# Reordering block work, low halves and merges in projection B and the output projection, and giving modulation chunks their own buffer

## The chip, the cores and the metric

The kernel runs on one core of a Trainium2 chip. Its engines are TensorE (matmuls; PE in the profile, with PEld for weight loads), VectorE (DVE), ScalarE (ACT), GpSimd (POOL) and SyncE (SP), which issues most of the loads. The metric is the device time of one execution in microseconds. Lower is better.

## What is computed

One decoder block on a sequence of 512 rows with 1024 columns, in float32: a modulation vector, one wide input projection, two mixers (a gated MLP over chunks, and sparse attention), each with a projection, a merge, an output projection, and a SwiGLU FFN.

```python
mod = silu(c) @ w_ada + b_ada                 # shift1, scale1, gate1, shift2, scale2, gate2
h = rms_norm(x, norm1_g) * (1 + scale1) + shift1
a_u, a_v, q, k, v, qi, ki, wi, g_a, g_b = split(h @ w_in)
y_a = chunked_gmlp(gelu(a_u), gelu(a_v), ...)
y_b = dsa_attention(q, k, v, qi, ki, wi)      # top-k keys per query, softmax, values
merged = sigmoid(g_a) * (y_a @ w_proj_a) + sigmoid(g_b) * (y_b @ w_proj_b)
x = x + gate1 * (merged @ w_out)
h2 = rms_norm(x, norm2_g) * (1 + scale2) + shift2
f_g, f_u = split(h2 @ w_ffn_in)
x = x + gate2 * ((silu(f_g) * f_u) @ w_ffn_out)
return rms_norm(x, final_norm_g)
```

## The kernel before

**Split products.** Every float32 product is made of three matmuls on rounded parts: high x high, high x low, low x high (mm3, L51 to L55). So each weight block that arrives has its high half made by a ScalarE copy and its low half by a subtraction, mostly on VectorE. These two steps are the "prep" of a block (L95).

**The stream.** Weight blocks ("w") and modulation chunks ("m") stand in one hand-written list, `stream`. A chunk is 512 KB of w_ada, used by two VectorE products that add to an accumulator (mac, L171); four chunks make half a section, and 24 chunks (numbered 0 to 23 here) the three sections 2, 3 and 4. When a half is complete, sec_tasks (L364) makes its column sum: for sections 3 and 4 four transposes on TensorE, then a reduction and one or two tiny steps on VectorE (L383 to L393). ensure(upto) (L119) issues the loads of as many blocks ahead as room(i) allows, and preps up to the block named; get(i, ahead=2) preps two weight blocks beyond the one that is about to be used. Weight blocks land in a buffer with three slots (tag raw). Chunks land there too, except those marked mid, which have a buffer with one slot, the tile mraw with tag A2. Each engine takes its instructions in program order, and a tile that is to be written waits until the last reader of the tile that had the buffer before is done, even where that reader stands later in the program.

**The stages around the change**, in order of time: projection A (W_GA and W_PA: gate and projection groups 0 to 3 of mixer A, two blocks to a group), the attention loop with the gate groups W_GB in its gaps, projection B (W_PB, opt_b with pb_evac: groups PB0 to PB3 of two blocks each), the output projection, the second norm and the FFN.

**Output projection.** Its first half of the inner dimension is done as a seven-product scheme over blocks: the merged rows' blocks and their sums (A11, A12, A22, S1 to S4 in part[0], made by o_sum and split by o_m), and w_out's blocks and differences (B11, B12, B21, B22, T1 to T4, loaded by o_issue into oraw, made by o_sub and split by o_w). The list O_STEPS says which of these steps is done at each of the eight blocks of projection B; o_step runs one entry. The products (oprod, L1300) then run with bank copies between: seed copies an accumulator to a new bank, keep copies it to SBUF, add_kept adds it back. The second half of the inner dimension (W_O[0] to W_O[3], tile wx for the first two) follows as plain products, half of the rows after the other (L1335). W_O[0] and W_O[1] lie in the buffers of yb, the input of projection B.

**Second norm.** resid adds to the residual rows and squares them; row_rstd and norm2_x normalise two row blocks, one on VectorE and one on ScalarE (tile xn); norm2_T transposes them on TensorE (x2T), scales (h2f) and splits them (h, in HB). norm2_T(0) serves the first half of the rows, norm2_T(1) the second; the latter stands inside the first FFN group (tile pf), whose two weight columns are W_F[0] and W_F[1], four blocks together (WF0[0] to WF0[3]). s_issue(-2) and s_prep(-2) load and prepare the weights of the first of the later FFN groups; s_prep gives four pairs of a ScalarE step and VectorE steps (a0, d0 to a3, d3), named pre[0] to pre[3]. t_diff and t_split follow.

Of the kernel before, what the change touches and what calls it, by code (L numbers as in the profile page):

```python
# [9 lines left out]
F32 = mybir.dt.float32  # L10
# [6 lines left out]
S = 512  # L17
# [11 lines left out]
def block_kernel(ctx: ExitStack, tc: tile.TileContext, x, positions, w_ada, b_ada, w_in,  # L29
# [28 lines left out]
    stream, wseq, chunk = [], [], {}  # L58
# [7 lines left out]
        return len(stream) - 1  # L66

    def add_m(dma, fn, early=False, mid=True):
        stream.append(dict(kind="m", fn=fn, dma=dma, early=early, mid=mid and not early))
        return len(stream) - 1  # L70

    def issue(i):
        e = stream[i]
        if e["kind"] == "m" and e["early"]:
            k = mrot[0]
            mrot[0] += 1
            raw = s2pair(k % 8, F32).rearrange("p a n -> p (a n)")
        elif e["kind"] == "m" and e["mid"]:
            raw = mid.tile([128, 1024], F32, name="mraw", tag="A2", bufs=1)
        else:  # L80
            raw = base.tile([128, 1024], F32, name="raw", tag="raw", bufs=RAWB)
        e["raw"] = raw
        if e["kind"] == "m":
            e["dma"](raw)
            return
        k0, nk, n = e["kts"][0], len(e["kts"]), e["n"]
        src = e["src"][k0 * 128:(k0 + nk) * 128, :]
        e["view"] = lambda t: t[:, :nk * n].rearrange("p (j n) -> p j n", j=nk)
        v = e["view"](raw)
# [54 lines left out]
    def get(i, ahead=2):  # L144
        k = wseq.index(i)
        ensure(wseq[min(k + ahead, len(wseq) - 1)])
        return chunk[i]
# [75 lines left out]
                        sec_done.append((sec, half, tick[0] + 2, ah))  # L223
                yield dma, fn

    def group(src, c0, n=256, K=8, mods=None, pool=False, where=None, nm=1, mraw=True):
        ids = []
        for k0 in range(0, K, 4):
            ids.append(add_w(src, list(range(k0, min(K, k0 + 4))), c0, n,
                             P if pool == 2 or pool and k0 % 8 == 0 else V, where.pop(0) if where else None))  # L230
            for _ in range(nm):
                m = next(mods, None) if mods is not None else None
                if m is not None:
                    add_m(*m, mid=mods is mm_ and mraw)
        return ids
# [18 lines left out]
    W_GA, W_PA = [], []  # L254
    for g in range(4):
        W_GA.append(group(w_in, 4168 + 256 * g, mods=mm_, pool=2))
        W_PA.append(group(w_pa, 256 * g, mods=mm_ if g < 3 else None, pool=2))
    W_GB = [group(w_in, 5192 + 256 * g, pool=2 * (g == 1), mods=mm_ if g > 1 else None, mraw=False) for g in range(4)]
    stream[W_GB[1][0]]["lo"] = V
    W_PB = [group(w_pb, 256 * g, mods=mm_ if g < 3 else None, mraw=False) for g in range(4)]  # L260

    W_O = [add_w(w_o, [k0, k0 + 1], 512 * h, 512, V, where) for h, k0, where in
           ((0, 4, ("S2_2", "S2_3")), (0, 6, ("S2_6", "S2_7")), (1, 4, None), (1, 6, None))]
# [403 lines left out]

    qf = [base.tile([128, 2, S], F32, name=f"qf{g}", tag=f"X{g}", bufs=1) for g in range(4)]

    def opt_b(ids, K, rhs, banks, evac, per_chunk=None, post=None, midway=None):  # L670
        pb = [bank(b, "pb") for b in banks]
        for i in ids:
            if per_chunk:
                per_chunk()
            hi, lo = get(i)
            kts = stream[i]["kts"]
            for j, kt in enumerate(kts):
                for m in range(2):
                    cc = slice(m * 128, (m + 1) * 128)
                    mm3(pb[m], (hi[:, j, cc], lo[:, j, cc]), rhs[kt], kt == 0, kt == K - 1)  # L680
                if midway and j == 1:
                    midway()
            if i == W_PB[3][-1]:
                sec_tasks(True)
            if i == ids[-1]:
                evac(pb)
            if post:
                post()
            sec_tasks()
# [381 lines left out]

    mT, om, ow, oraw = {}, {}, {}, {}
    OM = {"A11": 0, "S1": 1, "S2": 2, "A12": 3, "S3": 0, "S4": 1, "A22": 2}
    OW = {"B11": ("k_hi", "k_lo"), "T1": ("v_hi", "v_lo"), "T2": ("G0", "G1"), "T4": ("k_hi", "k_lo")}

    def o_issue():
        for n, (name, kh, h) in enumerate((("B11", 0, 0), ("B12", 0, 1), ("B22", 1, 1), ("B21", 1, 0))):
            t = oraw[name] = mid.tile([128, 2, S], F32, name="oraw", tag=f"A{n}", bufs=1)
            SY.dma_start(t, w_o[kh * 256:kh * 256 + 256, h * 512:h * 512 + 512].rearrange("(j p) n -> p j n", p=128))

    def o_w(key, src):
        if key in OW:
            ow[key] = tuple(mid.tile([128, 2, S], F32R, name="ow", tag=t, bufs=1) for t in OW[key])
        else:
            ow[key] = tuple(base.tile([128, 2, S], F32R, name=t, tag=t, bufs=3) for t in ("hi", "lo"))
        split(*ow[key], oraw[src])

    def o_sub(o, a, b):
        V.tensor_sub(oraw[o], oraw[a], oraw[b])
# [6 lines left out]
    def o_m(key):  # L1096
        om[key] = tuple(base.tile([128, 2, 256], F32R, name="om", tag=f"S1_{OM[key] + 8 * e}", bufs=1) for e in range(2))
        split(*om[key], m_block(key))

    def o_sum(key):  # L1100
        if key == "S1":
            V.tensor_add(m_block("S1"), m_block("A21"), m_block("A22"))
        else:
            a, b = {"S2": ("S1", "A11"), "S4": ("A12", "S2"), "S3": ("A22", "S2")}[key]
            V.tensor_sub(m_block(key), m_block(a), m_block(b))

    def pb_evac(g):
        def ev(pb):
            for m in range(2):
                k = 2 * g + m  # L1110
                t, o = t512("mg"), part[k // 4][:, k % 4]
                V.tensor_mul(t, pb[m], gbt[g][:, m])
                V.tensor_add(o, o, t)
                if k >= 4:
                    mT[k] = tuple(base.tile([128, S], F32R, name="mt", tag=f"S1_{k + 8 * e}", bufs=1) for e in range(2))
                    A.activation(mT[k][0], o, AF.Copy)
            for k in range(2 * g, 2 * g + 2):
                if k >= 4:
                    V.tensor_sub(mT[k][1], part[1][:, k % 4], f(mT[k][0]))
        return ev  # L1120

    O_STEPS = [[lambda: o_w("B11", "B11")],
               [lambda: o_sub("B11", "B12", "B11"), lambda: o_w("T1", "B11")],
               [lambda: o_sub("B11", "B22", "B11"), lambda: o_sub("B12", "B22", "B12")],
               [lambda: o_sum("S1"), lambda: o_m("A11"), lambda: o_sum("S2"), lambda: o_m("S1"),
                lambda: o_w("T2", "B11")],
               [lambda: o_m("S2"), lambda: o_m("A12"), lambda: o_sum("S4")],
               [lambda: o_sum("S3")],
               [lambda: o_w("B21", "B21")], []]

    def o_step():
        for fn in O_STEPS.pop(0):
            fn()

    mbank[0] = 5
    o_issue()
    for g in range(4):
        opt_b(W_PB[g], 8, yb, ((2, 3), (0, 1), (6, 7), (0, 1))[g], pb_evac(g), None, o_step)
    sec_tasks(True)


# [167 lines left out]

    WF0 = W_F[0] + W_F[1]  # L1310
    oprod(0, "A11", "B11", True)
    o_w("T3", "B12")
    seed(O, OB, 1, 0)
    oprod(3, "S1", "T1", True)
    o_m("S3")
    keep(O, 3, None)
# [549 lines left out]
```

## Time and profile before

| | |
|---|---|
| three runs | 844.22, 846.72, 849.07 us; median 846.72 |
| profiled execution | 844.57 us; span from first to last instruction 842.8 us |
| busy in the span | PE 822.8, PEld 731.1, DVE 679.4, ACT 410.0, POOL 107.9 us |
| moved by DMA | 109.10 MB, mean 129 GB/s |
| projection B | TensorE from 396.1 to about 444 us of the span |
| output projection | to about 491 us |
| second norm and first FFN group | to about 518 us |

The profile is of one execution, and its times are microseconds from the span's start. In a row of a timeline stand start, duration, engine, line, operation, output and inputs with their shapes, the count, and in square brackets how long the engine had been idle and which engine's step ended that. In a row of the windows stand the stretch, its length, the busy time of each engine with its count of instructions, the granted TensorE clock and the share and rate of DMA. In a row of grouped lines the numbers behind the bar are the busy time in us, the mean duration in ns, and the idle time ahead of the group. In the list of waits they are the total in us, the number of waits and the longest. An engine that isn't the bottleneck may idle at no cost.

### The profile page before, as it was taken

The page shows a single profiled execution, that of the slowest core. Times are in us where ns is not written, and L with a number is a line of the kernel's source. Part 1 is how long each engine was busy: PE and PEld are TensorE (multiplying, and loading weights), DVE is VectorE, ACT ScalarE, POOL GpSimd, SP SyncE. Part 2 cuts the span into 40 slices and gives each one's busy share as a digit, 9 for nine tenths or more (in the row PEclk, how much of TensorE's full clock was granted, in tenths as well). Part 3 has the DMA queues.
Part 4 walks back from the last instruction along what each step waited for, and adds up shares of the span by engine and source line. Part 5 has one row for each costly group of instructions (what it writes and reads, how often), then busy time and mean ns, then how long its engine had stood idle before and what let it go on. Part 6 is the DMA issues. An engine that isn't in the chain of part 4 may idle for free.

```text
span 842.8 us, 12864 instructions
## 1 busy us (share of the span) xinstructions
PE 822.8 (98%) x4980; PEld 731.1 (87%) x4980; DVE 679.4 (81%) x1169; ACT 410.0 (49%) x714; POOL 107.9 (13%) x101
## 2 busy tenths in 40 slices
PE   7999999999999999999988999999999999999996
PEld 6888889988888888988866889999999999888885
DVE  7978799798899648886787779889998888985635
ACT  6664445322332236666335466555555555563322
POOL 2060022452353411000000000000000000000001
PEclk9999999999999999999999999999999999999998
DMA  9962262432345541056641402345543334142212
GB/s 300 310 186 79 87 200 77 126 100 83 120 141 186 196 150 51 26 190 196 209 131 51 150 26 76 102 153 165 168 160 104 101 100 149 52 145 98 83 50 100
DMA packets 95677, 109.10 MB, mean 129 GB/s; under 512 B 5616, under 2 KB 76272, under 8 KB 95616
## 3 DMA queue, kind: packets, MB, share of 16 engines
q1 hardware_dynamic: 92512, 101.37, 38.8%
q0 software_dynamic: 2384, 6.10, 2.0%
q8 instruction: 39, 0.64, 0.3%
q10 hardware_dynamic: 720, 0.82, 0.3%
q14 instruction: 22, 0.18, 0.1%
HBM read 105.90 MB, written 2.10 MB: 128 GB/s over the span
## 4 chain that ended last, share of the span: by engine, by line
PE 85%; DVE 8%; ACT 2%; DMA 2%; issue 1%; SPq 0%; POOL 0%; POOLq 0%; DVEq 0%; ACTq 0%
PE R L53 7%; PE pb L55 7%; PE R L54 7%; PE pb L53 7%; PE R L55 7%; PE pb L54 7%; PE pfo L55 4%; PE pfo L54 4%; PE pfo L53 4%; PE pav L54 2%; PE pav L53 2%; PE pav L55 2%; PE pgb L53 2%; PE pgb L54 2%; PE pgb L55 2%
## 5 line engine op out<-in xcount | busy, mean ns | idle before, releaser
L112 ACT ACTIVATE hi<-raw 128x1024 fp32r<-128x1024 f32 (+2 forms) x82 | 84.5, 1034 | 101.1 <-PE pfo L55 35.2
L116 DVE TENSOR_TENSOR lo<-raw,hi 128x1024 fp32r<-128x1024 f32 (+2 forms) x46 | 55.5, 1212 | 48.5 <-ACT hi L112 48.3
L116 POOL TENSOR_TENSOR lo<-raw,hi 128x1024 fp32r<-128x1024 f32 x29 | 72.9, 2517 | 127.6 <-ACT hi L112 122.0
L53 PE MATMUL pb<-h,hi 128*128 128x512 f32 x192 | 76.4, 398 | 0.0
L55 PE MATMUL pb<-h,lo 128*128 128x512 f32 x192 | 75.8, 395 | 0.0
L54 PE MATMUL pb<-hl,hi 128*128 128x512 f32 x192 | 75.8, 395 | 0.0
L55 PE MATMUL pfo<-hi,gs 128*128 128x512 f32 (+1 forms) x126 | 46.4, 369 | 0.0
L54 PE MATMUL pfo<-lo,gs 128*128 128x512 f32 (+1 forms) x126 | 46.4, 368 | 0.0
L53 PE MATMUL pfo<-hi,gs 128*128 128x512 f32 (+1 forms) x126 | 46.4, 368 | 0.0
L53 PE MATMUL R<-tb,sx 128*128 128x256 f32 x160 | 45.3, 283 | 0.5 <-ACT R L1618 0.5
L53 PE MATMUL R<-tb,hi 128*128 128x256 f32 x160 | 44.9, 281 | 0.2 <-ACT ps L1636 0.2
L54 PE MATMUL R<-tb,sx 128*128 128x256 f32 x160 | 45.1, 282 | 0.0
L55 PE MATMUL R<-tb,sx 128*128 128x256 f32 x160 | 45.0, 281 | 0.0
L55 PE MATMUL R<-tb,lo 128*128 128x256 f32 x160 | 44.8, 280 | 0.0
L54 PE MATMUL R<-tb,hi 128*128 128x256 f32 x160 | 44.6, 279 | 0.0
L55 PEld LDWEIGHTS pb<-h,lo 128*128 128x128 f32 x192 | 36.0, 188 | 8.8
L54 PEld LDWEIGHTS pb<-hl,hi 128*128 128x128 f32 x192 | 36.0, 188 | 8.3
L53 PEld LDWEIGHTS pb<-h,hi 128*128 128x128 f32 x192 | 36.0, 188 | 8.3
L177 DVE SCALAR_TENSOR_TENSOR acc<-mraw,cols,acc 128x512 f32<-128x512 f32 x38 | 32.6, 859 | 8.2 <-DMA mraw<-in_w_ada_dram 7.5
L54 PE MATMUL pav<-lo,h 128*128 128x256 f32 x128 | 35.8, 279 | 0.0
L53 PE MATMUL pav<-hi,h 128*128 128x256 f32 x128 | 35.7, 279 | 0.0
L55 PE MATMUL pav<-hi,hl 128*128 128x256 f32 x128 | 35.7, 279 | 0.0
(400 smaller groups left out, 2663.9 us busy)
## 6 DMA issues: line engine op xcount, KB each, us to landing
raw<-in_w_ffn_in_dram SPq DMA_DIRECT2D x44, 512.0 KB, 4.3
raw<-in_w_in_dram SPq DMA_DIRECT2D x40, 512.0 KB, 3.8
mraw<-in_w_ada_dram SPq DMA_DIRECT2D x22, 512.0 KB, 3.8
raw<-in_w_ffn_out_dram SPq DMA_DIRECT2D x17, 512.0 KB, 3.6
s<-in_w_ada_dram SPq DMA_DIRECT2D x30, 256.0 KB, 5.6
raw<-in_w_ada_dram SPq DMA_DIRECT2D x10, 512.0 KB, 4.5
raw<-in_w_proj_a_dram SPq DMA_DIRECT2D x8, 512.0 KB, 4.6
raw<-in_w_proj_b_dram SPq DMA_DIRECT2D x8, 512.0 KB, 3.9
```

Of the source, the lines that this page charges most:

```text
L53: T.matmul(o, wh, rh, start=start, stop=False, **kw)
L54: T.matmul(o, wh, rlo, start=False, stop=False, **kw)
L55: T.matmul(o, wlo, rh, start=False, stop=stop, **kw)
L112: A.activation(hi[:, :m], e["raw"][:, :m], AF.Copy)
L116: e["lo"].tensor_sub(lo[:, :m], e["raw"][:, :m], f(hi[:, :m]))
L177: V.scalar_tensor_tensor(o, w, cs[:, j:j + 1], o, op0=OP.mult, op1=OP.add)
```

## The change

- Chunks: projection A takes two more (16 instead of 14). The attention loop keeps four. Projection B has four instead of six, after PB0's second block, both blocks of PB1 and PB2's first; these four land in the buffer of k_hi (free after the last score product), no longer in the three raw slots.
- opt_b gets a step that runs between the matmuls of a block and the merge (before, o_step ran behind the merge), and an ahead for get: 2 for PB0 to PB2, 0 for PB3, so that no w_out block of the plain part is prepped in projection B.
- o_issue takes names: B11, B12 and B22 load at the same place as before into A1, A0 and A2; B21 loads into k_hi in the fifth entry of O_STEPS. B11's and T4's halves lie in k_lo and A3.
- O_STEPS is regrouped: T1 has an entry of its own, T2 and the sum S1 come first in the fifth, A11, S2 and S1 in the sixth, A12 and B21 in the last.
- Output projection: the seed of accumulator 1 stands ahead of o_w("T3"); W_O[0] and W_O[1] are prepped ahead of the product S3 x T3, W_O[2] ahead of A22 x T4.
- Second norm: WF0[2] is prepped inside norm2_T(0), its low half one step later, followed by s_issue(-2). WF0[3] is prepped behind norm2_x(1), and pre[0], pre[1] and pre[2] all follow it.

```diff
-        stream.append(dict(kind="m", fn=fn, dma=dma, early=early, mid=mid and not early))
+        stream.append(dict(kind="m", fn=fn, dma=dma, early=early, mid=not early and mid))
...
-            raw = mid.tile([128, 1024], F32, name="mraw", tag="A2", bufs=1)
+            raw = mid.tile([128, 1024], F32, name="mraw", tag=e["mid"], bufs=1)
...
-            for _ in range(nm):
+            for _ in range(nm if isinstance(nm, int) else nm[k0 // 4]):
...
-    W_PA.append(group(w_pa, 256 * g, mods=mm_ if g < 3 else None, pool=2))
+    W_PA.append(group(w_pa, 256 * g, mods=mm_, pool=2))
...
-    W_PB = [group(w_pb, 256 * g, mods=mm_ if g < 3 else None, mraw=False) for g in range(4)]
+    W_PB = [group(w_pb, 256 * g, mods=mm_, nm=((0, 1), (1, 1), (1, 0), (0, 0))[g], mraw="k_hi") for g in range(4)]
...
-    def opt_b(ids, K, rhs, banks, evac, per_chunk=None, post=None, midway=None):
+    def opt_b(ids, K, rhs, banks, evac, per_chunk=None, post=None, midway=None, step=None, ahead=2):
...
-            hi, lo = get(i)
+            hi, lo = get(i, ahead)
...
+            if step:
+                step()
             if i == W_PB[3][-1]:
                 sec_tasks(True)
...
-    OW = {"B11": ("k_hi", "k_lo"), "T1": ("v_hi", "v_lo"), "T2": ("G0", "G1"), "T4": ("k_hi", "k_lo")}
+    OW = {"B11": ("k_lo", "A3"), "T1": ("v_hi", "v_lo"), "T2": ("G0", "G1"), "T4": ("k_lo", "A3")}
...
     O_STEPS = [[lambda: o_w("B11", "B11")],
-               [lambda: o_sub("B11", "B12", "B11"), lambda: o_w("T1", "B11")],
+               [lambda: o_sub("B11", "B12", "B11")],
+               [lambda: o_w("T1", "B11")],
                [lambda: o_sub("B11", "B22", "B11"), lambda: o_sub("B12", "B22", "B12")],
-               [lambda: o_sum("S1"), lambda: o_m("A11"), lambda: o_sum("S2"), lambda: o_m("S1"),
-                lambda: o_w("T2", "B11")],
-               [lambda: o_m("S2"), lambda: o_m("A12"), lambda: o_sum("S4")],
-               [lambda: o_sum("S3")],
-               [lambda: o_w("B21", "B21")], []]
+               [lambda: o_issue("B21"), lambda: o_sum("S1"), lambda: o_w("T2", "B11")],
+               [lambda: o_m("A11"), lambda: o_sum("S2"), lambda: o_m("S1")],
+               [lambda: o_m("S2"), lambda: o_sum("S4")],
+               [lambda: o_m("A12"), lambda: o_sum("S3"), lambda: o_w("B21", "B21")]]
...
-        opt_b(W_PB[g], 8, yb, ((2, 3), (0, 1), (6, 7), (0, 1))[g], pb_evac(g), None, o_step)
+        opt_b(W_PB[g], 8, yb, ((2, 3), (0, 1), (6, 7), (0, 1))[g], pb_evac(g), None, None, None, o_step,
+              2 if g < 3 else 0)
...
     oprod(0, "A11", "B11", True)
+    seed(O, OB, 1, 0)
     o_w("T3", "B12")
-    seed(O, OB, 1, 0)
...
     o_m("A22")
+    ensure(W_O[1])
     oprod(2, "S3", "T3", False)
     keep(O, 2, "acc")
     oprod(1, "S4", "B22", False)
-    ensure(W_O[1])
+    ensure(W_O[2])
     oprod(2, "A22", "T4", False)
...
     ensure(W_O[3])
     add_kept(O, 3, 2)
+    stream[WF0[2]]["lo"] = "later"
...
                 if (half, h, n_) == (0, 0, 0):
                     ensure(WF0[1])
-                if (half, h, n_) == (0, 1, 0):
-                    ensure(WF0[3])
-                    s_issue(-2)
                 if (half, h, n_) == (1, 1, 0):
-                    norm2_T(0)
-                    pre = s_prep(-2)
-                    for fn in pre[0]:
-                        fn()
+                    norm2_T(0, {1: [lambda: ensure(WF0[2])],
+                                2: [lambda: stream[WF0[2]]["do"](), lambda: s_issue(-2)]})
...
-    pre[1][0]()
     for e in range(2, 4):
         row_rstd(e)
     norm2_x(1)
-    pre[1][1]()
-    for fn in pre[2]:
+    ensure(WF0[3])
+    pre = s_prep(-2)
+    for fn in pre[0] + pre[1] + pre[2]:
         fn()
```

More of the change, by code (lines that the diff above doesn't have):

```diff
@@ L224, in mod_sec, with group @@
                 yield dma, fn
-    def group(src, c0, n=256, K=8, mods=None, pool=False, where=None, nm=1, mraw=True):
+    def group(src, c0, n=256, K=8, mods=None, pool=False, where=None, nm=1, mraw="A2"):
         ids = []
@@ L1073, in block_kernel, with o_issue @@
     OM = {"A11": 0, "S1": 1, "S2": 2, "A12": 3, "S3": 0, "S4": 1, "A22": 2}
-    OW = {"B11": ("k_hi", "k_lo"), "T1": ("v_hi", "v_lo"), "T2": ("G0", "G1"), "T4": ("k_hi", "k_lo")}
-    def o_issue():
-        for n, (name, kh, h) in enumerate((("B11", 0, 0), ("B12", 0, 1), ("B22", 1, 1), ("B21", 1, 0))):
-            t = oraw[name] = mid.tile([128, 2, S], F32, name="oraw", tag=f"A{n}", bufs=1)
+    OW = {"B11": ("k_lo", "A3"), "T1": ("v_hi", "v_lo"), "T2": ("G0", "G1"), "T4": ("k_lo", "A3")}
+    def o_issue(*which):
+        for name, kh, h, tag in (("B11", 0, 0, "A1"), ("B12", 0, 1, "A0"), ("B22", 1, 1, "A2"), ("B21", 1, 0, "k_hi")):
+            if name not in which:
+                continue
+            t = oraw[name] = mid.tile([128, 2, S], F32, name="oraw", tag=tag, bufs=1)
             SY.dma_start(t, w_o[kh * 256:kh * 256 + 256, h * 512:h * 512 + 512].rearrange("(j p) n -> p j n", p=128))
@@ L1135, in block_kernel @@
     mbank[0] = 5
-    o_issue()
+    o_issue("B11", "B12", "B22")
     for g in range(4):
-        opt_b(W_PB[g], 8, yb, ((2, 3), (0, 1), (6, 7), (0, 1))[g], pb_evac(g), None, o_step)
+        opt_b(W_PB[g], 8, yb, ((2, 3), (0, 1), (6, 7), (0, 1))[g], pb_evac(g), None, None, None, o_step,
+              2 if g < 3 else 0)
     sec_tasks(True)
```

## The prediction

> **What bounds the kernel now.** I read the head of the profile's page first, then the list of what TensorE waited for over the whole span.
>
> ```profile
> span 842.8 us, 12864 instructions
> PE 822.8 (98%) x4980; PEld 731.1 (87%) x4980; DVE 679.4 (81%) x1169; ACT 410.0 (49%) x714; POOL 107.9 (13%) x101
> PE warm L442 <- DMA cst<-in_consts_dram: 4.6, 1, 4.6
> PE pb L55 <- DVE lo L116: 2.4, 1, 2.4
> PE po L53 <- DVE Gc L391: 1.8, 1, 1.8
> PE po L53 <- ACT po L1286: 1.8, 1, 1.8
> PE x2T L1193 <- ACT xn L1172: 1.0, 1, 1.0
> ```
>
> TensorE is busy 98% of the span. Its longest wait is the start-up (4.6 us on the identity's load); of the rest nearly all lies in four waits of one stretch: projection B (tile pb), the output projection (po) and the transposes of the second norm (x2T). The change edits exactly this stretch, so the listed waits, 7.0 us, are the most it can win, unless it shortens matmul work, and it doesn't.
>
> The timeline of TensorE shows what the first three cost, and that of VectorE and ScalarE what was late.
>
> ```profile
> 430.11 0.40 PE L54 MATMUL pb<-yb,hi 128*128 128x512 f32 x1
> 432.86 0.51 PE L55 MATMUL pb<-yb,lo 128*128 128x512 f32 x1 [2.35 <-DVE lo L116]
> 445.19 0.39 PE L55 MATMUL po<-ow,om 128*128 128x512 f32 x1
> 447.38 0.47 PE L53 MATMUL po<-ow,om 128*128 128x512 f32 x1 [1.81 <-DVE Gc L391]
> 451.42 0.40 PE L55 MATMUL po<-ow,om 128*128 128x512 f32 x1
> 453.58 0.50 PE L53 MATMUL po<-ow,om 128*128 128x512 f32 x1 [1.76 <-ACT po L1286]
> ...
> 432.86:438.10 5.24, 5.24 (x23) 4.18 (x24) 5.17 (x8) 0.63 (x1) 0.00 (x0) 1.00 0.76 247
> ...
> 403.01 1.23 DVE L116 TENSOR_TENSOR lo<-raw,hi 128x1024 fp32r<-128x1024 f32 x1 [4.29 <-ACT hi L112]
> 398.74 8.05 DMA raw<-in_w_proj_b_dram
> 431.58 1.22 DVE L116 TENSOR_TENSOR lo<-raw,hi 128x1024 fp32r<-128x1024 f32 x1
> 441.50 1.06 ACT L112 ACTIVATE wx<-raw 128x1024 fp32r<-128x1024 f32 x1 [2.43 <-PE pb L55]
> 444.27 1.23 DVE L116 TENSOR_TENSOR wx<-raw,wx 128x1024 fp32r<-128x1024 f32 x1 [3.88 <-ACT hi L305]
> ```
>
> From the windows' row a 512-column matmul starts every 5.24/23 = 0.23 us. The steps across the three waits are 2.75, 2.19 and 2.16 us, so they lose 2.52 + 1.96 + 1.93 = 6.4 us.
>
> Their cause is one vector queue running late. The weights of projection B share three raw buffers with the modulation chunks, and one weight load went out only at 398.74 and took 8.05 us. VectorE, idle until the low half at 403.01, reaches that of the last group only at 431.58, while TensorE wanted it at 430.4: first wait. Then ScalarE stands at the high half of a w_out block (441.50), whose buffer yb still fills, and VectorE behind it until 444.27; the modulation reduction and the last merges come late: second and third wait.
>
> **Projection B in the new order.** Step costs come from the grouped rows of this stretch.
>
> ```profile
> L116 DVE TENSOR_TENSOR lo<-raw,hi 128x1024 fp32r<-128x1024 f32 x8 | 9.7, 1220 | 5.7 <-ACT hi L112 5.7
> L177 DVE SCALAR_TENSOR_TENSOR acc<-raw,cols,acc 128x512 f32<-128x512 f32 x9 | 6.7, 748 | 0.2
> L1089 DVE TENSOR_TENSOR oraw<-oraw 128x1024 f32<-128x1024 f32 x4 | 4.8, 1218 | 0.0
> L306 DVE TENSOR_TENSOR om<-part,om 128x512 fp32r<-128x512 f32 x7 | 4.7, 686 | 0.3 <-ACT om L305 0.3
> L1113 DVE TENSOR_TENSOR part<-part,mg 128x512 f32<-128x512 f32 x8 | 5.5, 693 | 0.3
> ...
> mraw<-in_w_ada_dram SPq DMA_DIRECT2D x22, 512.0 KB, 3.8
> ```
>
> The chunks leave the raw buffers, so weights land ahead; ScalarE's sigmoids still hold the first low half to 403.0. From there VectorE has, up to the low half of PB3's first block: five low halves and two w_out lows (7 x 1.2), three chunks of two products each (6 x 0.75), three w_out differences (3 x 1.2), two merges of four products (8 x 0.69). That is 8.4 + 4.5 + 3.6 + 5.5 = 22.0 us. One wait comes on top: the fourth chunk may load only when the third has left the single buffer, 3.8 us to land, of which 2.1 lie beside other vector work; I take 1.7. The low half is then ready at 426.7 instead of 432.8, TensorE wants it at about 430.4: margin 3.7 us, and the first wait goes. The blocks A11 to A12 (0.69 a half) fall into PB2 and PB3, where nothing else is left; the reduction moves ahead of the last group, the halves of w_out blocks 0 and 1 to just ahead of the fifth of the seven products. Walking on from 426.7: one sum and T2 (1.9), the last low half (1.2), A11, S2, S1 (2.1), the merge of PB2 with its two low halves (6 x 0.69), the reduction (1.0: a 512-column step and two tiny ones), four steps for S2, S4, A12, S3 (2.8) and B21 (1.2): 14.3 us, 441.0. TensorE leaves projection B at 444.0 (445.19 less five steps) - 2.5 = 441.5, so VectorE is free for the last merge at once. That merge (2.8), one 0.6 copy and the seed of the second accumulator, now ahead of T3, a pair of banks (1.06 as the 1024-column copy of 441.50), end near 446.0; its product comes after two products of 12 x 0.23, at 447.0. The tightest point is keep(2), which ScalarE makes behind T4, A22 and two w_out copies: from the difference for T4 (452.7 by the same walk) 1.06 + 0.6 + 2.1 + 1.06 = 457.5, wanted after six products at 458.1. So waits two and three go too: -6.4 us. Bounds: 0 to 1.0 us of new waits there; I take 0, since each margin is positive.
>
> At no cost: B21 loads later (SP, one DMA, wanted about 9 us after). The first chunk in k_hi waits on SP for the last score product, with a weight behind it that isn't wanted for some 20 us. No POOL queue is passed. The two chunks in projection A:
>
> ```profile
> 308.04 1.23 DVE L116 TENSOR_TENSOR lo<-raw,hi 128x1024 fp32r<-128x1024 f32 x1 [3.65 <-ACT hi L112]
> 313.29 0.69 DVE L963 CUSTOM_DVE_ANT_0 pt<-qk,sco 128x512 f32<-128x512 f32 x1 [4.02 <-PE qk L55]
> ```
>
> VectorE idles 3.65 and 4.02 us there, more than the four products of 0.75 (3.0 us); without that cover they would cost 3.0. The column sum of one section half (four small transposes, 1.0 us of VectorE) moves with them from projection B into the attention loop: nothing for TensorE.
>
> **The second norm in the new order.** Here the change puts work onto the path.
>
> ```profile
> 493.43 0.68 DVE L1255 TENSOR_TENSOR raw<-raw 128x512 f32<-128x512 f32 x1
> 495.36 0.69 DVE L1150 TENSOR_TENSOR rt<-po,gate1b 128x512 f32<-128x512 f32 x1
> 498.96 0.74 DVE L1174 TENSOR_SCALAR xn<-xr,sm 128x1024 f32<-128x1024 f32 x1
> 499.84 1.23 DVE L1264 TENSOR_TENSOR lo<-raw,hi 128x1024 fp32r<-128x1024 f32 x1
> 500.14 1.15 ACT L1172 ACTIVATE xn<-xr,sm 128x1024 f32<-128x1024 f32 x1 [0.34 <-POOL sm L1156]
> 501.20 1.04 ACT L1269 ACTIVATE hi<-raw 128x1024 fp32r<-128x1024 f32 x1
> 503.42 0.99 DVE L1203 TENSOR_SCALAR h2f<-x2T,Gc 128x256 f32<-128x256 f32 x2
> 505.25 0.69 DVE L1208 TENSOR_TENSOR h<-h2f,h 128x512 fp32r<-128x512 f32 x1 [0.85 <-ACT h L1205]
> 505.89 0.28 PE L53 MATMUL pf<-h,wx 128*128 128x256 f32 x1
> 506.00 0.38 PE L54 MATMUL pf<-h,wx 128*128 128x256 f32 x1
> ```
>
> TensorE's matmul of 506.00 is the second of the half of the FFN group that reads the second norm's later rows. It runs 0.38 us against 0.28, started as its low half (505.25 + 0.69 = 505.9) became ready: there is no slack. Whatever delays VectorE's first step of that norm (503.42) delays TensorE as much.
>
> Before: from the normalised rows (498.96) to that step 4.46 us, for L1264, L1265, L1272 (3.58 from 499.84 on). After: ensure(WF0[3]) and all of pre[0] to pre[2] stand between. ScalarE makes the high half of WF0[3] only behind its own row block, which waits for POOL: it began its next copy 2.24 us after 498.96, and a copy takes 1.04, so VectorE stands until 3.3 us. Then the low half, 1.2; pre[0], 495.36 - 493.43 = 1.93; the same 3.58. Sum 10.0, or 5.5 more. Against this the rows come earlier: pre[0] no longer precedes the residual (-1.9), but WF0[2]'s copy (1.04) and low half (1.2) now sit inside the first half's norm, and its last step waits for ScalarE. Walked through, the residual starts at 494.9 instead of 495.36: -0.5; bounds -1.9 and +0.5. Net +5.0 at 506.00. The wait for x2T falls by the 0.5, but that only makes the wait behind it longer: some 5.2 us at one place.
>
> **Sum.** -6.4 + 5.0 = -1.4 us. The profiled execution took 844.57 (span 842.8 and 1.8 around it), so 843.2; the median of the three runs is 846.72, hence 845.3. Half a per cent, 4.2 us, is about what a measurement of this kernel can tell from no change.
>
> **The rivals.** (1) The clock. Four short waits become one long one. After the start-up's 4.6 us of waiting the first matmuls ran slowly:
>
> ```profile
> 4.60:6.00 1.40, 1.39 (x6) 1.40 (x7) 1.00 1.12 353
> 6.00:8.00 2.00, 2.00 (x12) 2.00 (x11) 1.00 1.05 396
> 9.00:10.00 1.00, 1.00 (x12) 1.00 (x11) 1.00 1.00 372
> ```
>
> 18 matmuls in 3.4 us, then 12 in each 1.0 us: at the full rate those 18 take 1.5, so 1.9 us were lost, though the column of the granted clock says 1.00 throughout. Against it: behind the wait of 2.35 us above, the pace was full at once (23 in 5.24 us). A wait of 5.2 us lies nearer the 4.6. If it slows TensorE the same way: 845.3 + 1.9 = 847.2. [...]
>
> (2) The wait isn't paid. If VectorE fills the moved work into its gaps (rows earlier by the bound of 1.9, not 0.5, and no standing for WF0[3]'s high half, 3.3 - 0.74 = 2.6), the loss is 5.0 - 1.4 - 2.6 = 1.0: 846.72 - 6.4 + 1.0 = 841.3. It is faster from where the loss is under 2.2. For it: only the order of two queues, read from the program, puts the 2.6 us there. Against it: each engine took its instructions in program order in every row above.
>
> (3) Slower: the single buffer in k_hi. Each chunk's load starts when the chunk before it is used up. If a landing takes the 8.05 us seen above instead of 3.8, three loads and products in a row take 3 x (8.05 + 1.5) = 28.7 from 398.4, to 427; 1.2 + 2.4 + 2.8 + 1.2 of VectorE follow before PB3's low half, 434.6, and TensorE stands 4.2 us for it, with some 1.8 more in the output projection, whose margins were 1 us. Of the 6.4 us 0.4 stays: 846.72 - 0.4 + 5.0 = 851.3. It decides from a landing of about 6 us. For it: four w_out blocks load at that time. Against: they now go out staggered, one of them 30 us later.
>
> **How the numbers follow.** The forecast (845.3) gets 0.36, rival 1 0.22, rival 2 0.26, rival 3 0.16. Faster by over 0.5% is rival 2, 0.26; slower rival 3, 0.16; the other two lie within, 0.58. The range goes from 840.0 (rival 2 with a loss near zero) to 850.0: it takes in the bounds of 1.0 for the output projection and 3.0 for the chunks on top of rival 1's side, and leaves out most of rival 3.
>
> **What would show it.** Right: no wait of TensorE above 0.5 us on pb or po; x2T's about 0.5; one of about 5 us on pf for h, between the two halves; VectorE idle about 2.6 us ahead of the low half of WF0[3], then seven steps before the first h2f. Rival 1: 256-column matmuls 0.24 us apart behind that wait instead of 0.12. Rival 2: no wait on pf. Rival 3: waits of VectorE on DMA of the chunks and TensorE waits on pb. The forecast is wrong if pb and po keep over 2 us of waits, or pf's wait is under 3 or over 7.

## The result, and the profile after

The changed kernel takes 844.1 us (median of 20 runs, 843.31 to 845.24), the kernel before 847.0 in the same set (844.22 to 849.07): a ratio of 0.9967, 95% interval 0.9959 to 0.9975, or 2.8 us. Forecast were 845.3 and no difference above 0.5%. The profiled execution took 843.38 us, against 844.57 before: only 1.2 us less.

The first line of the profile's page of the changed kernel:

```profile
span 841.6 us, 12868 instructions
```

The list of TensorE's waits, in full (us in total, count, longest):

```profile
PE warm L442 <- DMA cst<-in_consts_dram: 4.8, 1, 4.8
PE pf L53 <- ACT h L1210: 4.3, 1, 4.3
PE x2T L1198 <- ACT xn L1177: 0.8, 1, 0.8
PE modS L415 <- DVE accw L177: 0.2, 1, 0.2
```

The three waits on pb and po (6.0 us) are gone, and so are two small ones on R (0.5 and 0.2, not shown in the prediction). A new one stands on pf: 4.3 us (forecast some 5.2) for the upper half of h. VectorE's timeline shows why the first three went (four rows of projection B) and why the new one came (three of the second norm):

```profile
418.01 1.54 DVE L177 SCALAR_TENSOR_TENSOR acc<-mraw,cols,acc 128x512 f32<-128x512 f32 x2 [1.92 <-DMA mraw<-in_w_ada_dram]
425.52 1.22 DVE L116 TENSOR_TENSOR lo<-raw,hi 128x1024 fp32r<-128x1024 f32 x1
438.91 1.22 DVE L306 TENSOR_TENSOR lo<-oraw,hi 128x1024 fp32r<-128x1024 f32 x1
440.80 0.69 DVE L1116 TENSOR_TENSOR mg<-pb,gb 128x512 f32<-128x512 f32 x1 [0.66 <-PE pb L55]
...
488.09 0.68 DVE L1155 TENSOR_TENSOR rt<-po,gate1b 128x512 f32<-128x512 f32 x1
495.01 1.23 DVE L116 TENSOR_TENSOR wx<-raw,wx 128x1024 fp32r<-128x1024 f32 x1 [2.57 <-ACT wx L112]
501.61 0.99 DVE L1208 TENSOR_SCALAR h2f<-x2T,Gc 128x256 f32<-128x256 f32 x2
```

The wait for the fourth chunk is 1.92 us (forecast 1.7). The low half of PB3's first block is ready at 425.52 + 1.22 = 426.7 (forecast 426.7). B21's low half ends at 440.1 (forecast 441.0), and VectorE then stands 0.66 us for TensorE, not TensorE for it.

In the second norm VectorE stands 2.57 us for the high half of WF0[3] (forecast 2.6). TensorE's timeline at the new wait:

```profile
503.46 0.58 PE L53 MATMUL pf<-h,wx 128*128 128x256 f32 x1 [4.31 <-ACT h L1210]
504.19 0.58 PE L54 MATMUL pf<-h,wx 128*128 128x256 f32 x1
504.56 0.41 PE L55 MATMUL pf<-h,wx 128*128 128x256 f32 x1
...
508.19 0.35 PE L54 MATMUL pf<-h,wx 128*128 128x256 f32 x1
```

And the windows' row behind it (length; PE, PEld, DVE, ACT, POOL busy with counts; granted clock; DMA):

```profile
505.00:508.00 3.00, 3.00 (x16) 3.00 (x16) 2.14 (x5) 2.92 (x6) 0.00 (x0) 0.50 0.01 3
```

Behind the wait of 4.31 us the matmuls start 0.21 us apart (17 steps from 504.56 to 508.19) instead of 0.12, until about 508.4, and here the granted clock shows it: 0.50 from 505 to 508. (A row of the windows counts every matmul that touches its stretch, so its 16 is more than started in it.) That was the first rival.

TensorE's groups by tile, which give its landmarks (nanoseconds shortest/median/longest, first and last start). The kernel before:

```profile
L53 PE MATMUL pf<-h,wx x64: 277/282/388, 491.3 to 517.0; 128*128 128x256 f32 x64
L53 PE MATMUL R<-h,sa x80: 276/279/286, 517.3 to 709.7; 128*128 128x256 f32 x80
L55 PE MATMUL R<-tb,sx x160: 277/283/283, 529.4 to 718.6; 128*128 128x256 f32 x160
```

The changed kernel:

```profile
L53 PE MATMUL pf<-h,wx x64: 277/283/580, 484.4 to 517.0; 128*128 128x256 f32 x64
L53 PE MATMUL R<-h,sa x80: 276/279/286, 517.4 to 708.6; 128*128 128x256 f32 x80
L55 PE MATMUL R<-tb,sx x160: 277/283/283, 528.9 to 717.5; 128*128 128x256 f32 x160
```

| step of TensorE, us | before | after | change | forecast |
|---|---|---|---|---|
| first pf | 491.3 | 484.4 | -6.9 | -6.4 |
| from there to the 2nd matmul of the upper half (506.00; 504.19) | 14.7 | 19.8 | +5.1 | +5.0 |
| from there to the first R | 11.3 | 13.2 | +1.9 | 0 (rival 1: +1.9) |
| first to last R | 201.3 | 200.1 | -1.2 | 0 |
| rest | | | -0.1 | 0 |
| profiled time | 844.57 | 843.38 | -1.2 | -1.4 |

### The profile page after: what moved, and what is told of

Read it like the earlier page. It is cut to its first block, busy times and chain, and to the rows that moved or that the text cites. A ratio compares the mean times of both kernels' runs of the same rounds, so it can differ in the third digit from the quotient of the medians.

```text
span 841.6 us, 12868 instructions
## 1 busy us (share of the span) xinstructions
PE 824.3 (98%) x4980; PEld 733.8 (87%) x4980; DVE 678.3 (81%) x1169; ACT 410.7 (49%) x714; POOL 108.5 (13%) x101
## 4 chain that ended last, share of the span: by engine, by line
PE 94%; DVE 3%; ACT 1%; issue 1%; DMA 0%; POOL 0%; POOLq 0%
PE pb L53 9%; PE pb L55 9%; PE pb L54 9%; PE R L53 8%; PE R L54 8%; PE R L55 8%; PE pfo L55 4%; PE pfo L54 4%; PE pfo L53 4%; PE pav L54 2%; PE pav L53 2%; PE pav L55 2%; PE pgb L53 2%; PE pgb L54 2%; PE pgb L55 2%; PE po L54 2%
## 5 line engine op out<-in xcount | busy, mean ns | idle before, releaser
L177 DVE SCALAR_TENSOR_TENSOR acc<-mraw,cols,acc 128x512 f32<-128x512 f32 x49 | 39.8, 812 | 18.0 <-DMA mraw<-in_w_ada_dram 17.0
```

The costliest lines, as they stand in the source:

```text
L177: V.scalar_tensor_tensor(o, w, cs[:, j:j + 1], o, op0=OP.mult, op1=OP.add)
```

## The experiments

Each median is set against the kernel before in the same set (846.2 to 846.3 us).

**Which half of the change does what.** One kernel has all of the change but the second norm's part, one that part alone.

The first, against the changed kernel:

```diff
-    stream[WF0[2]]["lo"] = "later"
...
+                if (half, h, n_) == (0, 1, 0):
+                    ensure(WF0[3])
+                    s_issue(-2)
                 if (half, h, n_) == (1, 1, 0):
-                    norm2_T(0, {1: [lambda: ensure(WF0[2])],
-                                2: [lambda: stream[WF0[2]]["do"](), lambda: s_issue(-2)]})
+                    norm2_T(0)
+                    pre = s_prep(-2)
+                    for fn in pre[0]:
+                        fn()
...
+    pre[1][0]()
...
-    ensure(WF0[3])
-    pre = s_prep(-2)
-    for fn in pre[0] + pre[1] + pre[2]:
+    pre[1][1]()
+    for fn in pre[2]:
         fn()
```

The second takes the same lines the other way round into the kernel before.

> The changed kernel with the second norm's part of the change undone: WF0[2] and WF0[3] prepped after the third plain block, pre[0] inside the first half's norm, pre[1] and pre[2] around norm2_x(1), as before. Theory (order of the queues): the three waits on pb and po stay away, the wait on pf for h goes, x2T's wait is back at about 1 us, the clock stays at 1.00 in 480 to 511. Time: 847.0 - 6.4 = 840.6, ratio to before 0.992. Rival (VectorE is the last in 480 to 530 whatever the order): TensorE arrives earlier and waits there instead, 2 us or more on pf or R, time 842 to 844.

> The kernel before with the second norm's part of the change alone. Theory (order of the queues): the three waits of 2.4, 1.8 and 1.8 us stay, and a wait of 4 to 5 us on pf for h comes on top: 847.0 + 5.0 = 852.0, ratio 1.006; with the clock halved behind the wait up to 2.4 more. Rival (the moved steps fill gaps of VectorE, and the wait on pf comes from TensorE's earlier arrival alone): the wait on pf is under 1.5 us and the time within 1 us of before.

The front alone takes 837.58 us, ratio 0.9899 (0.9885 to 0.9912); the norm's part alone 852.09, ratio 1.0076 (1.0063 to 1.0089). So the change is a gain of 8.6 us and a loss of 5.9, which together give about the 2.8 measured, and without its second part it is faster than both kernels. The loss is as expected; the front's time lies 3.0 us below the 840.6 expected, and its 8.6 is more than the 7.0 us of waits that the prediction took for the most that can be won. Between the profiled executions the front wins 844.57 - 837.56 = 7.0 us; the last experiments come back to the rest. The longest of TensorE's waits behind the start-up, with the front alone:

```profile
PE x2T L1198 <- ACT xn L1177: 1.1, 1, 1.1
```

And the two longest with the norm's part alone:

```profile
PE pf L53 <- ACT h L1205: 4.3, 1, 4.3
PE pb L55 <- DVE lo L116: 2.4, 1, 2.4
```

The front alone has no wait left on pb, po or pf; the norm's part alone has the new 4.3 us beside the old ones.

**Which part of the front.** The chunks alone (counts, buffer k_hi, tags), and the order alone (O_STEPS, step, ahead, the moved halves and seed), both with before's second norm.

The entry of O_STEPS in which they differ, first chunks alone, then order alone:

```diff
-               [lambda: o_sum("S1"), lambda: o_m("A11"), lambda: o_sum("S2"), lambda: o_m("S1"),
+               [lambda: o_issue("B21"), lambda: o_sum("S1"), lambda: o_m("A11"), lambda: o_sum("S2"), lambda: o_m("S1"),
                 lambda: o_w("T2", "B11")],
...
+               [lambda: o_sum("S1"), lambda: o_w("T2", "B11")],
+               [lambda: o_m("A11"), lambda: o_sum("S2"), lambda: o_m("S1")],
```

> The kernel before with the chunks' part alone: two more chunks in projection A, four in projection B through the buffer of k_hi, the w_out blocks in the tags that this needs; the lists of steps, the prep of w_out's plain blocks and the second norm as before. Theory (the first wait comes from the shared raw buffers, the other two from ScalarE and VectorE standing at the high half of a w_out block whose buffer yb still fills): the wait on pb for the low half goes (2.4 us to under 0.5), the two on po stay at 2.5 to 4 us together, 2.0 to 3.5 us below the kernel before (842.8 to 844.3). Rival (VectorE was late by its load alone): with the chunks gone all three waits go, 6 us or more below, 840.

> The kernel before with the order alone: the regrouped list of steps, run ahead of the merge, no w_out prep in projection B's last group, the halves of w_out at their new places, the seed ahead of T3; chunks, their buffers and the second norm as before. Theory: the wait on pb stays (1.8 to 3 us), the two on po go (under 1 us together), 3 to 4 us below the kernel before (842.5 to 843.5). Rival (the new order alone lifts VectorE's load ahead of the low half far enough): all three go, 840 or less. Second rival (the raw slots that w_out's blocks now hold longer make loads late): waits on po or R stay above 2 us, time as before.

Chunks alone: 842.20 us, ratio 0.9956 (0.9942 to 0.9970), 0.6 us below the range expected. Order alone: 838.18 us, ratio 0.9907 (0.9894 to 0.9920), nearly the whole gain of the front. The order was expected to keep the wait on pb; it has none on pb or po, as its first rival said. VectorE's timeline of the kernel before, ahead of the low half of 431.58:

```profile
426.46 0.69 DVE L1102 TENSOR_TENSOR part<-part 128x512 f32<-128x512 f32 x1
...
430.14 1.53 DVE L177 SCALAR_TENSOR_TENSOR acc<-raw,cols,acc 128x512 f32<-128x512 f32 x2
```

With the order alone, that low half:

```profile
427.19 1.22 DVE L116 TENSOR_TENSOR lo<-raw,hi 128x1024 fp32r<-128x1024 f32 x1
```

With the chunks alone, that low half and the one of w_out's block:

```profile
429.23 1.22 DVE L116 TENSOR_TENSOR lo<-raw,hi 128x1024 fp32r<-128x1024 f32 x1
...
441.73 1.22 DVE L116 TENSOR_TENSOR wx<-raw,wx 128x1024 fp32r<-128x1024 f32 x1 [2.69 <-PE pb L55]
```

Between the two rows of before lie S1, A11, S2, S1's split and T2: 430.14 - 426.46 = 3.7 us. The order alone puts them behind the low half, which comes 4.4 us earlier; the chunks alone bring it 2.35 us forward. Either is enough for the first wait. TensorE's timeline and a row of the windows with the chunks alone:

```profile
450.03 0.50 PE L53 MATMUL po<-ow,om 128*128 128x512 f32 x1 [2.80 <-ACT po L1288]
```

```profile
452.00:456.00 4.00, 4.00 (x19) 3.27 (x18) 2.96 (x3) 2.45 (x5) 0.00 (x0) 1.00 0.00 0
```

The wait for the reduction is gone, but one of 2.80 us for the copy of an accumulator stays, since ScalarE (until 438.95, not shown) and VectorE (until 441.73) still stand at the block whose buffer yb fills. Of these two kernels only the order alone is rid of that wait.

**What the clock costs behind the long wait.** Zeros keep TensorE busy where it waits, 60 and then 36 matmuls of them; the changed kernel itself ran beside the second. (The tile zero is made once at the start.)

```diff
             if half == 0 and w == 1:
+                for _ in range(60):      # 36 in the second kernel
+                    T.matmul(pf[1][1][:, 256:384], onesr, zero, start=False, stop=False, skip_group_check=True)
                 t_diff()
```

> The changed kernel with 60 matmuls on zeros (128 columns each, about 3.6 us) between the two halves of the first FFN group, added to a bank as zeros, where TensorE waits 4.3 us for h. Theory (the long wait halves the clock, which costs): granted clock 1.00 instead of 0.50 behind them, the group's second half 2.3 us shorter; the R stage then waits a little for VectorE as before, so 0.9 to 2.3 us gained: 841.8 to 843.2. Rival (the clock's loss is covered, since VectorE is late in this stretch anyway): 844.1 as the changed kernel, with waits on R instead. Should the zeros last longer than the wait, some tenths are lost again.

> The changed kernel with 36 matmuls of zeros between the two halves of the first FFN group; 60 of them had taken 6.81 us, so 36 take 4.1 and should end with the wait of 4.3 us instead of 2.5 us behind it. Theory (the clock falls because TensorE stands 4.3 us, and that costs some 2 us on top of the wait): granted clock 1.00 in 498 to 511 us, first matmul of R at 515.2 to 515.7 instead of 517.4, a time 1.0 to 2.0 us below the changed kernel's own in this set. Rival (what follows the wait is held by VectorE's and ScalarE's steps for R and not by the clock): clock 1.00 as well, but R at 517 and a time within 0.5 us of the changed kernel's.

> The changed kernel once more, as the yardstick for the 36 matmuls of zeros in the same set: 843.3 to 844.5 us, one wait of 4.3 us on pf, granted clock near 0.50 for some 4 us behind it, first matmul of R at 517.4. If the clock's fall is a matter of chance, its profile may show 1.00 behind the wait and R near 515.4.

With 60: 843.29 us, ratio 0.9966 (0.9953 to 0.9978). They took 6.81 us instead of the 3.6 expected, 2.5 more than the wait, and ate what they might have won, so this run decides nothing. With 36: 843.08, ratio 0.9966 (0.9953 to 0.9979), against 843.75, ratio 0.9975 (0.9963 to 0.9986), of the changed kernel. TensorE's timeline with the 36 zeros, the windows' row and the groups of R:

```profile
499.43 4.13 PE L1571 MATMUL pf<-zero,onesr 128*128 128x128 f32 x36
...
504.62 0.39 PE L54 MATMUL pf<-h,wx 128*128 128x256 f32 x1 [0.34 <-DVE h L1215]
```

```profile
505.00:508.00 3.00, 3.00 (x28) 3.00 (x27) 2.39 (x5) 2.88 (x5) 0.00 (x0) 1.00 0.01 3
```

```profile
L53 PE MATMUL R<-h,sa x80: 276/279/286, 516.0 to 708.4; 128*128 128x256 f32 x80
L55 PE MATMUL R<-tb,sx x160: 277/283/283, 528.0 to 717.3; 128*128 128x256 f32 x160
```

The same three views of the changed kernel in that set:

```profile
504.98 0.57 PE L54 MATMUL pf<-h,wx 128*128 128x256 f32 x1 [0.34 <-DVE h L1213]
```

```profile
505.00:508.00 3.00, 3.00 (x14) 3.00 (x15) 2.40 (x5) 2.84 (x6) 0.00 (x0) 0.50 0.00 0
```

```profile
L53 PE MATMUL R<-h,sa x80: 276/279/286, 517.9 to 709.1; 128*128 128x256 f32 x80
L55 PE MATMUL R<-tb,sx x160: 277/283/283, 529.4 to 718.0; 128*128 128x256 f32 x160
```

From the second matmul of the upper half to the first R it takes 516.0 - 504.62 = 11.4 us with the zeros, the 11.3 of the kernel before, and 12.9 without: the fall costs 1.5 us there (1.9 in the first profile of the changed kernel). The stage R then takes 201.3 us with the zeros and 200.1 without: 1.2 come back, of which two waits on R (0.5 and 0.2) explain 0.7, and the rest stays open. The times differ by 0.67 us; the runs of the two kernels overlap (842.80 to 843.99, and 843.58 to 844.23), so this net figure is an indication. At its place the cost of the fall is shown (1.5 us); at the end of the kernel little of it is left.

**Which step of the second norm.** One kernel moves WF0[3] alone into norm2_T(0), one puts WF0[2] and WF0[3] with their load back to before's places and leaves only pre[0] behind the rows.

The first, and then the second, against the changed kernel:

```diff
-                                2: [lambda: stream[WF0[2]]["do"](), lambda: s_issue(-2)]})
+                                2: [lambda: stream[WF0[2]]["do"](), lambda: s_issue(-2)],
+                                3: [lambda: ensure(WF0[3])]})
...
-    ensure(WF0[3])
```

```diff
-    stream[WF0[2]]["lo"] = "later"
...
+                if (half, h, n_) == (0, 1, 0):
+                    ensure(WF0[3])
+                    s_issue(-2)
                 if (half, h, n_) == (1, 1, 0):
-                    norm2_T(0, {1: [lambda: ensure(WF0[2])],
-                                2: [lambda: stream[WF0[2]]["do"](), lambda: s_issue(-2)]})
+                    norm2_T(0)
...
-    ensure(WF0[3])
```

> The changed kernel with one step moved: WF0[3] is prepped in the last step of norm2_T(0) instead of behind norm2_x(1). Theory (order of the queues): VectorE's idle 2.6 us ahead of that low half goes and the low half (1.2) no longer stands between norm2_x(1) and norm2_T(1), while the rows come 1.2 to 1.5 us later; the wait on pf falls from 4.3 to about 2, the clock stays at 1.00 behind it: 844.1 - 2.4 = 841.7, or 840.8 if the clock's loss counts as well. Rival (the wait on pf is not due to WF0[3] but to pre[0] to pre[2] alone): the wait stays above 3.5 us and the time at 844.

> The changed kernel with the blocks WF0[2] and WF0[3] and the load for the first later FFN group back at the places of before; only the first pair of that group's preparation stays behind the second norm's rows. By the prediction's terms the standing for WF0[3]'s high half (2.6 us) and its low half (1.2) go, VectorE stands some 1.5 us for the first copy of the pair instead, and the pair's 1.9 us are balanced by the residual that starts 1.9 earlier: a wait on pf of 1.0 to 2.0 us, no fall of the clock, 838.5 to 840. Rival (the pair is the larger part, since its copy stands behind ScalarE's row block): a wait of 3 us or more, the clock falls, 842 or more.

WF0[3] early: 842.84 us, ratio 0.9965 (0.9951 to 0.9979). The new place has a standing of its own, and VectorE's timeline has one more behind the rows:

```profile
488.30 1.23 DVE L116 TENSOR_TENSOR wx<-raw,wx 128x1024 fp32r<-128x1024 f32 x1 [1.65 <-ACT wx L112]
490.04 0.68 DVE L1155 TENSOR_TENSOR rt<-po,gate1b 128x512 f32<-128x512 f32 x1
496.53 0.69 DVE L1261 TENSOR_TENSOR sa<-raw,sa 128x512 fp32r<-128x512 f32 x1 [1.54 <-ACT sa L1257]
501.40 0.99 DVE L1208 TENSOR_SCALAR h2f<-x2T,Gc 128x256 f32<-128x256 f32 x2
```

It stands 1.65 us for the same high half, the residual starts at 490.04 instead of 488.09, then it stands 1.54 for pre[0]'s copy: the first h2f comes at 501.40 instead of 501.61. TensorE's wait for the upper half falls to 2.5 us, but the new standing costs it 1.3 us in the lower half, ahead of 490.18, and the clock still falls behind (0.50 from 506 to 508). Neither expectation was met; moving that block alone moves the standing, not the end.

Pre late: 839.62 us, ratio 0.9921 (0.9907 to 0.9934), as expected. VectorE's timeline, TensorE's, and the windows:

```profile
492.84 0.69 DVE L1261 TENSOR_TENSOR sa<-raw,sa 128x512 fp32r<-128x512 f32 x1 [1.54 <-ACT sa L1257]
```

```profile
499.56 0.58 PE L53 MATMUL pf<-h,wx 128*128 128x256 f32 x1 [2.04 <-ACT h L1210]
```

```profile
500.00:502.00 2.00, 1.85 (x9) 1.71 (x9) 1.82 (x5) 1.87 (x4) 0.00 (x0) 0.50 0.00 0
```

The standing of 1.54 us and a wait on pf of 2.04 are what was expected (2.0 was its upper end). So WF0[2] and WF0[3] with their load made 2.3 of the 4.3 us of the wait, and the place of pre[0], with the ScalarE step of pre[1] that moved along, the rest. Not as expected: the clock fell here too, behind a wait of 2.04.

**Why the measured gain is over twice the profiled one.** The kernel before once more, and with 20 matmuls of zeros in the place of its wait on pb.

```diff
             hi, lo = get(i)
+            if i == W_PB[3][0]:
+                for _ in range(20):
+                    T.matmul(pb[0][:, :128], onesr, zero, start=True, stop=True)
```

> The kernel before once more, for a second profile. Theory of the clock: if its time is above 846, its granted clock is near 0.50 for 4 to 6 us behind the wait on pb, and po starts about 2 us later than 444.0; if it is near 844.5, 1.00 and 444.0. Rival (landing times): clock 1.00 in both cases, and a time above 846 goes with a longer wait on pb or po.

> The kernel before with 20 matmuls of zeros ahead of projection B's last group, 0.114 us each, 2.3 us together, in the place of the wait of 2.4 us on pb. The profile of before took 844.57 us and showed clock 1.00 behind that wait, its runs have a median of 846.2 to 847.0; the second profile of the same stretch (the second norm alone) showed 0.50 for 6 us behind it. Theory (in most runs the clock falls behind this wait and costs about 2 us): median 844.0 to 844.8, the spread of the runs under 1.5 us instead of 3 to 5, clock 1.00 in 430 to 448. Rival (the runs differ because loads land at different times): median 846 and more, spread as before.

The second profile of the kernel before took 846.53 us. TensorE's timeline at the wait on pb, a row of the windows, and the group that gives po's first matmul:

```profile
433.48 0.80 PE L55 MATMUL pb<-yb,lo 128*128 128x512 f32 x1 [2.36 <-DVE lo L116]
```

```profile
434.00:436.00 2.00, 2.00 (x6) 1.54 (x5) 2.00 (x4) 0.00 (x0) 0.00 (x0) 0.50 0.83 290
```

```profile
L53 PE MATMUL po<-ow,om x16: 392/394/628, 446.0 to 468.8; 128*128 128x512 f32 x16
```

The same group in the first profile of the kernel before:

```profile
L53 PE MATMUL po<-ow,om x16: 392/399/502, 444.0 to 466.8; 128*128 128x512 f32 x16
```

The kernel with zeros, TensorE's timeline and the windows:

```profile
447.85 0.47 PE L53 MATMUL po<-ow,om 128*128 128x512 f32 x1 [1.81 <-DVE Gc L393]
```

```profile
434.00:436.00 2.00, 2.00 (x10) 1.65 (x9) 2.00 (x3) 0.00 (x0) 0.00 (x0) 1.00 0.77 279
448.00:452.00 4.00, 4.00 (x11) 3.14 (x12) 3.93 (x7) 0.69 (x2) 0.00 (x0) 0.57 0.58 198
```

The wait on pb is as long as in the first profile (2.36, then 2.35 us), but the clock behind it is 0.50. From the end of that wait to po's first matmul it takes 446.0 - 433.48 = 12.5 us instead of 444.0 - 432.86 = 11.1: 1.4 us for the clock. The other 0.6 of the 2.0 by which po starts later came ahead of the wait, whose low half was itself 0.62 later; that part fits the rival, loads that land at other times (an earlier low half, whose block waits for its load, comes at 408.59 instead of 407.97). Behind the wait for the reduction the clock fell once more in this execution (450.21 to 453.63), and the wait for the copy shrank from 1.76 to 0.2 us, so that from po's first matmul on nothing more was lost. The 1.96 us between the two times (846.53, 844.57) are these 2.0. With the zeros (2.34 us of them) the clock is 1.00 at that place, and the median is 845.03 us (11 runs, 844.33 to 847.85) against 846.26; but the ratio is 0.9992 (0.9981 to 1.0002), the spread didn't shrink to 1.5 us, and behind the next wait (1.81 us, for the reduction) the clock fell to 0.50 for 3.4 us (0.57 is the mean of the row). So what is shown is that the first profiled run of before was one of its fastest, and that in another one a fall of the clock makes up 1.4 of the 2.0 us between them.

For the median there is an indication. Of the 36 runs of the kernel before beside the experiments, the 11 with the highest mean granted clock (0.997; the mean also counts a fall at the kernel's end, 0.50 from 840 to 842.8 in the first profile) took 845.0 us on average, the other 25 (0.993 to 0.996) 846.5. The eight runs of the front alone and of the order alone, which keep none of the three waits, have a mean clock of 0.997 to 0.999, and each of these kernels' runs lie within 0.9 us. So about 1.5 us of the kernel before's median go with falls of the clock behind its waits; that they cause all of it isn't shown.

**When the clock fell.** The lengths of the waits alone don't decide it. Rows of the windows: the kernel before at its wait on pb, its second profile at the same wait (three rows), and the changed kernel at its long one.

```profile
430.00:434.00 4.00, 1.65 (x7) 1.03 (x7) 3.96 (x7) 1.70 (x3) 0.00 (x0) 1.00 0.25 81
...
430.00:434.00 4.00, 1.25 (x3) 0.80 (x4) 3.96 (x6) 2.32 (x4) 0.00 (x0) 0.89 0.12 23
434.00:436.00 2.00, 2.00 (x6) 1.54 (x5) 2.00 (x4) 0.00 (x0) 0.00 (x0) 0.50 0.83 290
436.00:440.00 4.00, 4.00 (x17) 3.21 (x17) 3.83 (x7) 1.27 (x2) 0.00 (x0) 0.93 0.62 209
...
498.00:503.00 5.00, 1.15 (x10) 0.94 (x8) 4.57 (x6) 1.85 (x3) 0.00 (x0) 0.85 0.26 90
```

In the first profile the clock stays at 1.00 through the wait of 2.35 us and behind it. In the second it is 0.50 behind one of 2.36, for about 3.4 us (0.89 and 0.93 are the means of rows in which it changes). In the changed kernel it is 0.50 from 501.50, inside the wait, to 508.33. Behind the wait for the reduction it stayed at 1.00 in the first profile and fell in the second and with the 20 zeros, after 1.81 us each time; behind 2.04 us (pre late) it fell, behind 2.80 (chunks alone) it didn't. So from its length alone it can't be said whether a wait of 2 to 3 us costs the clock, and what decides it isn't shown by these runs. A wait of 4.3 us on pf halved it in all three profiles that have one: 0.50 from 505 to 508 in both of the changed kernel, and from 516 to 518 with the norm's part alone.

## Why the prediction was right, and where its steps were not

The range (840 to 850) and the likeliest class (within 0.5%) held, and 844.1 lies 1.2 us from the 845.3. By its own steps:

- **Three waits go, -6.4.** Right: -6.9 at the first pf. The margin of 3.7 us for PB3's first low half, the wait on the chunk and the walk through the two queues held within 1 us.
- **Their cause.** Incomplete. The late weight load and the shared raw buffers were put first. Giving the chunks their own buffer does remove the first wait, but so does the order alone without touching the buffers, since 3.7 us of other steps stood ahead of that low half. The cause named for the second and third (ScalarE at a w_out block whose buffer yb still fills) is borne out for the third: with the chunks alone VectorE's low half of that block still starts only at 441.73, and a wait of 2.80 us stays.
- **The second norm costs +5.0.** Right: +5.1 at the matmul it was worked out for, and the norm's part alone costs 5.9 us of time. Its terms held too: 2.57 for 2.6 of standing; the first h2f 17.2 us after the first pf (501.61 - 484.4) instead of 12.1.
- **The sum left the clock out.** This is the step that failed: the forecast took the first rival (0.22) as not happening. It happened in both profiles of the changed kernel, for 1.9 and 1.5 us (the clock was halved for 6.83 us in the first and for 3.4 in the second), where the start-up rows had given 1.9. The argument against it, that behind 2.35 us the pace was full at once, rested on one execution: in another one of the same kernel the clock was 0.50 behind 2.36 us at the same place. The start-up rows show the same pace: in that profile the clock's record begins at 8.62 us, so the 1.00 ahead of it is no measurement, and the matmuls start 0.21 us apart until then and 0.11 behind.
- **What came back.** No case had it: 1.2 us in R, 0.7 of it two waits for ScalarE that are gone once TensorE comes later. The two omissions, +1.9 and -1.2, and the 0.5 by which the front won more, nearly cancel, which is why -1.4 fitted the profiled pair's -1.2. That closeness is luck.
- **The base.** The forecast carried the 2.15 us between profile and median over unchanged. The changed kernel's median lies only 0.7 above its profile. Its one long wait costs the clock in both profiles; the kernel before paid for a shorter one in the second profile and not in the first. The measured 2.8 exceeds 1.4 through this base. That the clock is the larger part of it is shown for one execution, and the 36 runs point the same way. For the same reason the 7.0 us of listed waits weren't the most that could be won: what the clock loses behind them, in the runs where it falls (1.4 us in the second profile of the kernel before), goes too.
- **Rivals.** The second (the wait isn't paid) fell with the 4.3 us, the third with the chunk's 1.92 us of wait at one place.

## What to carry to other kernels

Cost the two ends of a change apart: here a reordering that wins 8 us stood beside one that gives 6 back, and undoing the second is the fastest version that ran (the order alone is 0.6 us behind, with overlapping intervals). A step moved behind another engine's copy costs the standing for that copy too, not only its own length: 2.57 us here for a low half of 1.2. Short waits cost the clock in some executions (2.36 us in the second profile of the kernel before; 2.35 in the first didn't); a wait of 4.3 us cost it in each of three profiles. When a profile of the kernel before lies at the low end of its runs, look at a second profile before a difference of a few us is explained.

## What the runs showed of the hardware

- In these runs the granted clock didn't follow the length of a wait alone. One of 2.35 us left it at 1.00 in one execution of the kernel before, and one of 2.36 halved it in another; one of 1.81 left it at 1.00 in the first and halved it in the second; it fell behind 2.04 (pre late), and behind 2.80 it didn't (chunks alone, 1.00 in 448 to 460).
- A wait of 4.3 us halved it in both profiles of the changed kernel (4.31 us in the first) and with the norm's part alone. It was 0.50 for 6.83 us in the first profile of the changed kernel, and for about 3.4 in the second and in the second of the kernel before.
- 36 zero matmuls of 128 columns, each with a weight load, took 4.13 us, 0.115 each, while those of 256 columns start 0.12 apart: half the columns weren't faster.
